# Borders between the sub-layers of a four-layer trunk on one core: order of conditioning and weight work, buffers of the last weights, engine of one split

## The chip, the cores and the metric

One core of a Trainium2 chip runs the whole program in one launch. The metric is the time of one execution on the device in microseconds (us). Engines are named as in the profile: PE (TensorE matmuls; PEld its weight loads), DVE (VectorE), ACT (ScalarE), POOL (GpSimd) and SP (the queue that issues the DMAs here).

## The reference

Four layers on x of 512 tokens by 1024 features. Each layer has two sub-layers f, a token mixer (convolution module, gated linear recurrence, matrix memory, stick-breaking attention, one kind per layer) and a gated ConvFFN with 2816 hidden features. Each is applied as

```
h = x * (1 + scale) + shift
x <- LayerNorm(alpha * x + (1 + gate) * f(h))
```

Shift, scale and gate are columns of `silu(c) @ ada_w[i] + ada_b[i]`, 6 x 1024 numbers for each layer, from one conditioning vector c. All is in fp32.

## The kernel before

The rows of x lie in four tiles X[0..3] of 128 tokens by 1024 (t is the row block). Precision comes from splitting each operand into a high part (`fp32r`, cast by ACT) and a low part (the difference, by DVE), and adding three products on PE: high*high, low*high, high*low.

**Weights.** `unit` (L223) loads one 512 KB piece of weights into one of three `raw` buffers by a DMA on SP, and `parts` (L239) splits it: ACT casts `whi` (L243), DVE subtracts `wlo` (L245). Both tags have WBUFS = 3 buffers for the whole program, so a fourth piece is cast only when PE is through with the first.

**The end of a sub-layer.** `down` (L317) is the last product. In its second half (h = 1) the last TAIL = 3 pieces are all loaded first (L362), and PE then goes row block by row block: 18 matmuls for t = 0, then for t = 1, 2 and 3, so that the norm of one row block runs while PE is at the next. For each row block `evict` (L556) does the norm: DVE adds the product to X (L567) and takes statistics (L568, L591, L592), POOL takes the power of -1/2 (L593), DVE finishes (L594), ACT normalises (L606, twice), and `make_h` (L484) makes the next sub-layer's h: PE transposes into PSUM (L492, tile `tr`, once for each half q of four 128-blocks), ACT (q = 0, L497) or DVE (q = 1, L500) applies scale and shift, ACT casts `hh` (L503), and the low part `hl` (L504) comes from POOL for q = 0 and from DVE for q = 1. The second norm of a layer and the first of the next are the same code, so there are seven such borders. The eighth end, the output, has no next sub-layer.

**The start of the next one.** The four FFNs and the matrix memory begin with `up_head` (L276): three pieces of weights, each multiplied first with the columns of t = 0 and 1 (24 matmuls of 256 columns), then, all three again, with those of t = 2 and 3. After them `up` (L286) takes one piece at a time. The recurrence and the attention begin with `down(..., head=HEAD)`, which takes t = 0, 1 of three pieces and then t = 2, 3. The recurrence ends in `down_late` (L368), a different form of the last product: one piece of each half is left for the end.

**Conditioning.** `ada_unit` (L204) loads one 512 KB piece of ada_w into a buffer of tag `araw` (four of them) and reduces it against silu(c) on DVE (L209); `fill` (L212) calls it, mostly once for each `up`. FFN 0 holds 56 such units, FFN 1 and 2 hold 48 each, for the layer after.

**Order.** A scheduler puts every engine's instructions into one fixed order before the run, by priorities (`unit` has a raised one), data dependences and a model of durations. An engine executes in that order, so an instruction whose operand is late holds up all that follows on its engine. `tc.issue_after(z)` adds an edge of order, without a semaphore, from z to each instruction traced in the block on z's engine; DMAs on SP are not bound by it.

Of the kernel before, what the change touches and what calls it, by code (L numbers as in the profile page):

```python
# [10 lines left out]
F32 = mybir.dt.float32  # L11
F32R = mybir.dt.float32r
AF = mybir.ActivationFunctionType
ALU = mybir.AluOpType
PSUM = bass.MemoryType.PSUM

P = 128
D = 1024
T = 512
KD = D // P  # L20
# [3 lines left out]
NF = D_FF // P  # L24
# [12 lines left out]
WPRIO = 150  # L37
# [11 lines left out]
FB = 4  # L49
WBUFS = 3  # L50
TAIL = 3
# [92 lines left out]
class Trunk:  # L144
    def __init__(self, ctx, tc, ins, out):
        self.ctx, self.tc, self.nc, self.ins, self.out = ctx, tc, tc.nc, ins, out
        nc = self.nc
        E = ctx.enter_context
        self.const = E(tc.tile_pool(name="const", bufs=1))
        self.wp = E(tc.tile_pool(name="wp", bufs=2))  # L150
        self.xp = E(tc.tile_pool(name="xp", bufs=1))
        self.sp = E(tc.tile_pool(name="sp", bufs=2))
        self.ps = E(tc.tile_pool(name="ps", bufs=1, space=PSUM))
        self.psum(mm="012345", tr="67")
        self.ident = self.const.tile([P, P], F32, name="ident")
        nc.sync.dma_start(out=self.ident, in_=ins["ident"])
        self.ones = self.const.tile([P, 1], F32, name="ones")
        nc.vector.memset(self.ones, 1.0)
        self.onesr = self.const.tile([P, P], F32R, name="onesr")
        nc.vector.tensor_copy(self.onesr, self.ones.broadcast_to([P, P]))  # L160
        self.mhalf = self.const.tile([P, 8], F32, name="mhalf")
        nc.vector.memset(self.mhalf, -0.5)
        self.sbc = self.const.tile([P, D], F32, name="sbc")
        cb = self.wp.tile([P, D], F32, tag="raw", bufs=3, name="cb")
        nc.sync.dma_start(out=cb, in_=ins["c"].broadcast_to([P, D]))
        nc.scalar.activation(out=self.sbc, in_=cb, func=AF.Silu)
        self.X = [self.xp.tile([P, D], F32, name=f"X{t}") for t in range(NT)]
        self.par = {}
        self.adac = {}
        self.ada_q = []  # L170
        self.pre = {}
        self.apool = None
        self.started = False
        self.due = None

    def load_x(self):
        for t in range(NT):
# [34 lines left out]
    def fill(self, n=1):  # L212
        for _ in range(n):
            if self.apool is not None and self.ada_q:
                self.ada_unit(self.apool, self.abufs)

    def flush(self, i, upto, pool=None, bufs=None):
        pool = pool or self.apool
# [1 line left out]
            self.ada_unit(pool, bufs or self.abufs)  # L220


    def unit(self, w, u, name, gate=None, rowc=None, pool=None, bufs=WBUFS, prio=WPRIO):  # L223

        nc = self.nc
        pool = pool or self.wp
        with self.tc.high_priority(offset=prio):
            raw = self.wp.tile([P, D], F32, tag="raw", bufs=3, name=f"r_{name}_{u}")
            nc.sync.dma_start(out=raw, in_=w[u])
            if gate is not None:  # L230
                r = raw.rearrange("p (a c) -> p a c", a=2)
                gr = gate.rearrange("p (a c) -> p a c", a=1).broadcast_to([P, 2, T])
                if rowc is None:
                    nc.vector.tensor_tensor(out=r, in0=r, in1=gr, op=ALU.mult)  # L234
                else:
                    nc.vector.scalar_tensor_tensor(out=r, in0=r, scalar=rowc, in1=gr, op0=ALU.mult, op1=ALU.mult)
            return self.parts(raw, f"{name}_{u}", pool, bufs)

    def parts(self, raw, name, pool=None, bufs=WBUFS):  # L239
        nc = self.nc  # L240
        pool = pool or self.wp
        hi = pool.tile([P, D], F32R, tag="whi", bufs=bufs, name=f"wh_{name}")
        nc.scalar.copy(hi, raw)  # L243
        lo = pool.tile([P, D], F32R, tag="wlo", bufs=bufs, name=f"wl_{name}")
        nc.vector.tensor_tensor(out=lo, in0=raw, in1=hi.bitcast(F32), op=ALU.subtract)  # L245
        return hi, lo

# [28 lines left out]
    def up_head(self, w, us, name):  # L276

        hl = {}
        for u in us:
            hl[u] = self.unit(w, u, name)  # L280
            self.pre[u] = self.bank(f"p_{name}_{u}")
            self.up_mm(self.pre[u], hl[u], 0, T // 2)
        for u in us:
            self.up_mm(self.pre[u], hl[u], T // 2, T)

    def up(self, w, u, name, fills=1):  # L286
        if u in self.pre:
            ps = self.pre.pop(u)
        else:
            hl = self.unit(w, u, name)  # L290
            ps = self.bank(f"p_{name}_{u}")
            self.up_mm(ps, hl, 0, T)
        self.fill(fills)
        return ps
# [19 lines left out]

        return act

    def down(self, w, nk, act, name, halves, evict, head=0, tail=0, gate=None, rowc=None, early=0, turn=None):  # L317

        npair = nk // 2

        def load(h, kp):
            return self.unit(w, h * npair + kp, name, None if gate is None else gate[:, h * T:(h + 1) * T], rowc)

        def mm(bank, h, t, kp, hl, first, last):
            for a in range(2):
                ah, al = act(2 * kp + a, h)  # L330
                ts_ = slice(t * P, (t + 1) * P)
                wh, wl = (z[:, a * T:(a + 1) * T] for z in hl)
                for n, (l, r) in enumerate(((ah, wh), (al, wh), (ah, wl))):
                    self.nc.tensor.matmul(bank, l[:, ts_], r, start=(kp == first and a == n == 0),  # L334
                                          stop=(kp == last and a == 1 and n == 2))

        if early:
            hls = [load(0, kp) for kp in range(early)]
            for t0 in (0, 2):
                banks = [self.bank(f"pe_{name}_{t0 + t}") for t in range(2)]  # L340
                for kp in range(early):
                    for t in range(2):
                        mm(banks[t], 0, t0 + t, kp, hls[kp], 0, early - 1)
                for t in range(2):
                    evict(0, t0 + t, banks[t], True)
            self.psum(**turn)
        for h in range(halves):
            banks = [self.bank(f"p_{name}_{h}_{t}") for t in range(NT)]
            k0 = early if h == 0 else 0
            nh = head if h == 0 else 0  # L350
            nt = tail if h == halves - 1 else 0
            end = npair - 1
            hls = [load(h, kp) for kp in range(k0, nh)]
            for t0 in (0, 2):
                for kp in range(k0, nh):
                    for t in (t0, t0 + 1):
                        mm(banks[t], h, t, kp, hls[kp], k0, end)
            for kp in range(max(nh, k0), npair - nt):
                hl = load(h, kp)
                for t in range(NT):  # L360
                    mm(banks[t], h, t, kp, hl, k0, end)
            hls = [load(h, kp) for kp in range(npair - nt, npair)]  # L362
            for t in range(NT):
                for q, kp in enumerate(range(npair - nt, npair)):
                    mm(banks[t], h, t, kp, hls[q], k0, end)
                evict(h, t, banks[t])
# [117 lines left out]
    def make_h(self, n, t, G, B, name):  # L484

        nc = self.nc
        ts_ = slice(t * P, (t + 1) * P)
        for q in range(2):
# [4 lines left out]
            hf = self.sp.tile([P, 4, P], F32, tag="u", bufs=4, name=f"hf_{name}_{t}_{q}")  # L493
            for j in range(4):
# [4 lines left out]
                else:  # L499
                    nc.vector.tensor_scalar(out=hf[:, j, :], in0=ps[:, j * P:(j + 1) * P], scalar1=G[:, k:k + 1],  # L500
                                            scalar2=B[:, k:k + 1], op0=ALU.mult, op1=ALU.add)
            hh = self.hh[:, 4 * q:4 * q + 4, ts_]
            nc.scalar.copy(hh, hf)  # L503
            (nc.gpsimd if q == 0 else nc.vector).tensor_tensor(out=self.hl[:, 4 * q:4 * q + 4, ts_], in0=hf,  # L504
                                                               in1=hh.bitcast(F32), op=ALU.subtract)

    def first_h(self, i, w=None, us=(), name=None):

# [100 lines left out]
    def conformer(self, nxt):  # L609
# [9 lines left out]
        with tc.tile_pool(name="cf", bufs=1, reuse_waits="tile") as op, ExitStack() as es, \  # L619
# [70 lines left out]
            nc.sync.dma_start(out=bias, in_=ins["bpw2"].broadcast_to([P, D]))  # L690
            gate, evict = self.sub_end(cf, i, 0, nxt, bias)
            act = self.ring(cf, us, "cu", keep=True)
            self.down(ins["pw2"], KD, act, "pw2", 2, evict, tail=TAIL, gate=gate)


    def hgrn(self, nxt):
# [215 lines left out]
    def mlstm(self, nxt):  # L912
# [7 lines left out]
        with tc.tile_pool(name="mx", bufs=1, reuse_waits="tile") as mp, \  # L920
# [200 lines left out]
            with tc.tile_pool(name="mb", bufs=1, reuse_waits="tile") as bp:  # L1121
                self.psum(mm="012345", tr="67")
                gate, evict = self.sub_end(bp, i, 0, nxt, gate=gate)
                self.down(ins["mdn"], NM, self.ring(bp, xc, "mu"), "mdn", 2, evict, tail=TAIL, gate=gate)


    def stick(self, nxt):
# [4 lines left out]
        with tc.tile_pool(name="so", bufs=1, reuse_waits="tile") as op, ExitStack() as es:  # L1132
# [152 lines left out]
            for _, n, p in sorted((p + o, n, p) for p in range(KD) for n, o in STEPS.items()):  # L1285
# [2 lines left out]
            op = es.enter_context(tc.tile_pool(name="sf", bufs=1, reuse_waits="tile"))  # L1288
            gate, evict = self.sub_end(op, i, 0, nxt, gate=gate)
            self.down(ins["swo"], KD, lambda k, h: so[k], "swo", 2, evict, tail=TAIL, gate=gate,  # L1290
                      early=3, turn=dict(mm="012345", tr="67"))


    def ffn(self, i, nxt):
# [3 lines left out]
        with tc.tile_pool(name=f"g{i}", bufs=1, reuse_waits="tile") as gp:  # L1298
# [25 lines left out]
            self.flush(99, 0)  # L1324
            self.apool = None
            gate, evict = self.sub_end(gp, i, 1, nxt, gate=gate)
            self.down(dn_w, NF, self.ring(gp, gs, f"gr{i}"), f"d{i}", 2, evict, tail=TAIL, gate=gate)


@with_exitstack  # L1330
# [45 lines left out]
```

## Time and profile before

| | |
|---|---|
| median of 3 runs | 2791.32 us (2790.43 to 2795.23) |
| the profiled execution's own time | 2790.0 us |
| its span, first to last instruction | 2788.2 us |
| granted TensorE clock, mean over the span | 0.985 |
| busy: PE, DVE, ACT, POOL | 96%, 73%, 46%, 3% of the span |

Matmuls overlap in the records: one of 128x512 is shown as 0.39 us long and the next starts 0.23 us after it. So idle time of PE in the rows is shorter than the time that a wait costs. In the rows below, the text in square brackets is the engine's idle time just before the instruction and what ended it.

### The profile page before, as it was taken

To read this page: it belongs to the slowest core of one execution; us is meant where nothing else is said; L and a number is where in the kernel's file an instruction comes from. 1 tells how busy PE (TensorE), PEld (TensorE's weight loads), DVE (VectorE), ACT (ScalarE), POOL (GpSimd) and SP (SyncE) were. 2 spreads that over 40 slices of the span, in tenths; PEclk is the share of its full clock that TensorE was granted. 3 is DMA by queue.
4 is the path that set the end of the run, shared out by engine and by line. 5 is a ranking of instruction groups with operands and counts; after the bars stand their busy time and mean duration, and the time that the engine had idled before them with its cause. 6 is when DMAs were issued, how large, how long until landed. Compare 5 with 4: busy or idle time off the path is not lost. (4 is left out here: it accounts for less than half of the span.)

```text
span 2788.2 us, 33764 instructions
## 1 busy us (share of the span) xinstructions
PE 2669.6 (96%) x12980; PEld 2135.8 (77%) x12980; DVE 2031.1 (73%) x3105; ACT 1270.1 (46%) x1773; POOL 90.2 (3%) x108
## 2 busy tenths in 40 slices
PE   7979999999998899999999999999999999999998
PEld 5537888877775688887887777888887777788886
DVE  7557997664777699576766776997666588666676
ACT  3133433335674443333555543543334798443332
POOL 0001000000000100000000000100001000100000
PEclk9989999999999899999999999999999999999999
DMA  9834874323221485322322222774333211233222
GB/s 323 228 107 151 288 239 140 99 83 101 86 72 46 145 289 189 99 94 82 104 86 68 91 84 83 264 257 136 98 99 96 66 48 37 98 99 113 95 95 76
DMA packets 109673, 352.33 MB, mean 126 GB/s; under 512 B 12104, under 2 KB 22600, under 8 KB 109512
## 3 DMA queue, kind: packets, MB, share of 16 engines
q1 hardware_dynamic: 109512, 350.17, 38.2%
q8 instruction: 102, 1.67, 0.3%
q14 instruction: 59, 0.48, 0.1%
HBM read 341.63 MB, written 8.50 MB: 126 GB/s over the span
## 5 line engine op out<-in xcount | busy, mean ns | idle before, releaser
L273 PE MATMUL p_f<-hl,wh_f 128*128 128x512 f32 (+1 forms) x1504 | 567.9, 378 | 8.8 <-POOL hl L504 8.8
L273 PE MATMUL p_f<-hh,wh_f 128*128 128x512 f32 (+1 forms) x1504 | 566.0, 378 | 5.5 <-ACT hh L503 5.5
L273 PE MATMUL p_f<-hh,wl_f 128*128 128x512 f32 (+1 forms) x1504 | 565.8, 377 | 0.0
L243 ACT CAST wh_f<-r_f 128x1024 fp32r<-128x1024 f32 x176 | 185.1, 1053 | 337.6 <-PE p_f L273 330.5
L273 PEld LDWEIGHTS p_f<-hl,wh_f 128*128 128x128 f32 x1504 | 285.1, 190 | 61.8 <-POOL hl L504 10.9
L273 PEld LDWEIGHTS p_f<-hh,wh_f 128*128 128x128 f32 x1504 | 284.4, 190 | 57.8 <-ACT hh L503 6.4
L273 PEld LDWEIGHTS p_f<-hh,wl_f 128*128 128x128 f32 x1504 | 284.9, 190 | 51.5 <-issue 0.2
L245 DVE TENSOR_TENSOR wl_f<-r_f,wh_f 128x1024 fp32r<-128x1024 f32 x176 | 217.3, 1236 | 144.1 <-ACT wh_f L243 143.2
L209 DVE CUSTOM_DVE_ANT_0 ada<-ada,sbc,adab 128x1024 f32<-128x1024 f32 x192 | 243.1, 1275 | 9.1 <-DMA ada<-in_ada_dram 9.0
L1308 DVE SCALAR_TENSOR_TENSOR cg<-p_f,par,cg 128x511 f32<-128x511 f32 (+1 forms) x176 | 130.9, 744 | 2.7 <-ACT cg L1306 1.4
L1308 DVE SCALAR_TENSOR_TENSOR cv<-p_f,par,cv 128x511 f32<-128x511 f32 (+1 forms) x176 | 130.9, 744 | 1.5
L234 DVE TENSOR_TENSOR r_d<-r_d,gate 128x1024 f32<-128x1024 f32 x88 | 107.5, 1222 | 28.2 <-DMA r_d<-in_fdn_dram 27.3
L245 DVE TENSOR_TENSOR wl_d<-r_d,wh_d 128x1024 fp32r<-128x1024 f32 x88 | 107.5, 1221 | 27.4 <-ACT wh_d L243 27.4
L1318 ACT ACTIVATE cg<-cg 128x512 f32<-128x512 f32 x88 | 55.4, 629 | 146.6 <-DVE cg L1308 144.5
L273 PE MATMUL p_mup<-hh,wh_mup 128*128 128x512 f32 (+1 forms) x280 | 109.4, 391 | 0.9 <-ACT hf L497 0.9
L273 PE MATMUL p_mup<-hl,wh_mup 128*128 128x512 f32 (+1 forms) x280 | 108.0, 386 | 0.6 <-POOL hl L504 0.6
L273 PE MATMUL p_mup<-hh,wl_mup 128*128 128x512 f32 (+1 forms) x280 | 108.4, 387 | 0.0
L243 ACT CAST wh_d<-r_d 128x1024 fp32r<-128x1024 f32 x88 | 92.2, 1048 | 32.7 <-PE p_f L273 16.7
L593 POOL TENSOR_TENSOR mv<-mv,mhalf 128x1 f32<-128x1 f32 x32 | 21.9, 683 | 1852.1 <-DVE mv L592 1851.3
L606 ACT ACTIVATE X<-X,mv 128x512 f32<-128x512 f32 x56 | 42.6, 810 | 84.2 <-DVE mv L594 84.2
L1306 ACT ACTIVATE cg<-p_f,par 128x512 f32<-128x512 f32 x88 | 68.1, 774 | 14.9 <-PE p_f L273 14.9
L334 PE MATMUL p_d<-wl_d,gr2h 128*128 128x512 f32 x176 | 69.6, 396 | 0.0
(511 smaller groups left out, 5966.0 us busy)
## 6 DMA issues: line engine op xcount, KB each, us to landing
ada<-in_ada_dram SPq DMA_DIRECT2D x192, 512.0 KB, 4.6
r_f<-in_fup_dram SPq DMA_DIRECT2D x176, 512.0 KB, 3.5
r_d<-in_fdn_dram SPq DMA_DIRECT2D x88, 512.0 KB, 3.3
r_mup<-in_mup_dram SPq DMA_DIRECT2D x32, 512.0 KB, 3.3
r_pw<-in_pw_dram SPq DMA_DIRECT2D x24, 512.0 KB, 7.7
r_hqf<-in_hqf_dram SPq DMA_DIRECT2D x16, 512.0 KB, 3.3
r_mdn<-in_mdn_dram SPq DMA_DIRECT2D x16, 512.0 KB, 3.3
r_sqk<-in_sqk_dram SPq DMA_DIRECT2D x16, 512.0 KB, 3.7
```

Of the source, the lines that this page charges most:

```text
L209: nc.vector.tensor_tensor_reduce(out=raw, in0=raw, in1=self.sbc, scale=1.0, scalar=ab[:, j:j + 1], op0=ALU.mult, op1=ALU.add, accum_out=ac ...
L234: nc.vector.tensor_tensor(out=r, in0=r, in1=gr, op=ALU.mult)
L243: nc.scalar.copy(hi, raw)
L245: nc.vector.tensor_tensor(out=lo, in0=raw, in1=hi.bitcast(F32), op=ALU.subtract)
L273: self.nc.tensor.matmul(ps[:, c0:c1], a, b[:, k, c0:c1], start=(n == 0), stop=(n == 3 * KD - 1))
L334: self.nc.tensor.matmul(bank, l[:, ts_], r, start=(kp == first and a == n == 0), stop=(kp == last and a == 1 and n == 2))
L593: nc.gpsimd.tensor_tensor(out=mv[:, 2:3], in0=mv[:, 1:2], in1=self.mhalf[:, 0:1], op=ALU.pow)
L606: nc.scalar.activation(out=o[:, hs], in_=x[:, hs], func=AF.Identity, scale=mv[:, 2:3], bias=mv[:, 3:4])
L1306: nc.scalar.activation(out=o, in_=ps, func=AF.Identity, scale=w[2], bias=par[:, C_CONVB + m:C_CONVB + m + 1])
L1308: nc.vector.scalar_tensor_tensor(out=o[:, s:], in0=ps[:, :T - s], scalar=w[2 - s], in1=o[:, s:], op0=ALU.mult, op1=ALU.add)
L1318: nc.scalar.activation(out=cg, in_=cg, func=AF.Silu)
```

## The change

Four edits. (1) `make_h` does both low halves `hl` on DVE, and keeps the last cast and the last subtraction as `self.chain`. (2) `behind` opens `issue_after` for both; `fill` traces its ada units in it, and `up` the first three weight pieces that it splits itself after `up_head` (`late = 3`). So these are ordered on ACT and DVE after the last `make_h` step of the sub-layer before. (3) `down` takes `spare`: of the three tail pieces the second and third put their high and low parts into buffers of their own, in the FFNs the four `araw` buffers of 4 KB for each partition, in the convolution module, the matrix memory and the attention four new ones of tag `tw`. `down_late` has none. (4) `parts` takes the allocator `into` for that.

```diff
     def fill(self, n=1):
         for _ in range(n):
             if self.apool is not None and self.ada_q:
-                self.ada_unit(self.apool, self.abufs)
+                with self.behind():
+                    self.ada_unit(self.apool, self.abufs)
+    @contextmanager
+    def behind(self):
+        with ExitStack() as es:
+            for z in self.chain or ():
+                es.enter_context(self.tc.issue_after(z.ins))
+            yield
...
-        hi = pool.tile([P, D], F32R, tag="whi", bufs=bufs, name=f"wh_{name}")
+        tile_ = into or (lambda tag, nm: pool.tile([P, D], F32R, tag=tag, bufs=bufs, name=nm))
+        hi = tile_("whi", f"wh_{name}")
         nc.scalar.copy(hi, raw)
-        lo = pool.tile([P, D], F32R, tag="wlo", bufs=bufs, name=f"wl_{name}")
+        lo = tile_("wlo", f"wl_{name}")
...
         for u in us:
             self.up_mm(self.pre[u], hl[u], T // 2, T)
+        self.late = 3
     def up(self, w, u, name, fills=1):
...
-            hl = self.unit(w, u, name)
+            if self.late:
+                self.late -= 1
+                with self.behind():
+                    hl = self.unit(w, u, name)
+            else:
+                hl = self.unit(w, u, name)
...
-            hls = [load(h, kp) for kp in range(npair - nt, npair)]
+            hls = [load(h, kp, spare if kp > npair - nt else None) for kp in range(npair - nt, npair)]
...
-            nc.scalar.copy(hh, hf)
-            (nc.gpsimd if q == 0 else nc.vector).tensor_tensor(out=self.hl[:, 4 * q:4 * q + 4, ts_], in0=hf,
-                                                               in1=hh.bitcast(F32), op=ALU.subtract)
+            a = nc.scalar.copy(hh, hf)
+            b = nc.vector.tensor_tensor(out=self.hl[:, 4 * q:4 * q + 4, ts_], in0=hf, in1=hh.bitcast(F32), op=ALU.subtract)
+            self.chain = a, b
...
-            self.down(dn_w, NF, self.ring(gp, gs, f"gr{i}"), f"d{i}", 2, evict, tail=TAIL, gate=gate)
+            self.down(dn_w, NF, self.ring(gp, gs, f"gr{i}"), f"d{i}", 2, evict, tail=TAIL, gate=gate,
+                      spare=lambda tag, nm: gp.tile([P, D], F32R, tag="araw", bufs=FB, name=nm))
```

## Rows read from the trace of the kernel before

**Rows 1.** The page's first part: busy time and share of the span.
```profile
PE 2669.6 (96%) x12980; PEld 2135.8 (77%) x12980; DVE 2031.1 (73%) x3105; ACT 1270.1 (46%) x1773; POOL 90.2 (3%) x108
```
**Rows 2.** 40 us around each border: busy PE, PEld, DVE, ACT, POOL; PEclk; DMA.
```profile
238.00:278.00 40.00, 34.43 (x216) 30.32 (x215) 30.09 (x56) 21.41 (x38) 9.65 (x8) 0.96 0.49 171
614.00:654.00 40.00, 37.48 (x176) 29.50 (x175) 27.36 (x72) 24.60 (x41) 7.90 (x8) 1.00 0.26 82
931.00:971.00 40.00, 30.79 (x174) 26.73 (x174) 36.07 (x69) 18.45 (x34) 11.45 (x8) 0.83 0.54 183
1310.00:1350.00 40.00, 34.69 (x204) 30.14 (x203) 24.96 (x54) 21.44 (x38) 8.11 (x9) 0.91 0.20 65
1731.00:1771.00 40.00, 34.70 (x229) 30.45 (x229) 31.19 (x58) 22.86 (x39) 9.64 (x8) 1.00 0.50 174
2105.00:2145.00 40.00, 37.48 (x177) 29.80 (x176) 26.39 (x56) 23.68 (x40) 7.97 (x8) 1.00 0.28 84
2392.00:2432.00 40.00, 36.44 (x239) 32.08 (x238) 26.66 (x50) 25.11 (x42) 7.87 (x8) 1.00 0.27 94
```
**Rows 3.** Waits of PE, whole span: us in total, times, longest us.
```profile
PE tr L492 <- ACT X L606: 17.4, 20, 2.5
PE p_f L273 <- POOL hl L504: 8.8, 8, 1.6
PE p_f L273 <- ACT hh L503: 5.5, 4, 2.3
...
PE p_mup L273 <- ACT hf L497: 0.9, 1, 0.9
...
PE p_mup L273 <- POOL hl L504: 0.6, 1, 0.6
```
**Rows 4.** Timeline of PE at the fifth border: start us, length us.
```profile
1735.14 0.66 PE L492 MATMUL tr<-ident,X 128*128 128x128 f32 x4 [0.44 <-ACT X L606]
...
1741.22 0.39 PE L334 MATMUL p_mdn<-wh_mdn,muh 128*128 128x512 f32 x1
1741.45 0.40 PE L334 MATMUL p_mdn<-wh_mdn,mul 128*128 128x512 f32 x1
1742.73 0.66 PE L492 MATMUL tr<-ident,X 128*128 128x128 f32 x4 [0.89 <-ACT X L606]
...
1747.42 0.28 PE L273 MATMUL p_f<-hh,wh_f 128*128 128x256 f32 x1
1748.32 0.39 PE L273 MATMUL p_f<-hl,wh_f 128*128 128x256 f32 x1 [0.62 <-POOL hl L504]
...
1757.95 0.66 PE L492 MATMUL tr<-ident,X 128*128 128x128 f32 x4 [0.93 <-ACT X L606]
...
1760.85 0.62 PE L273 MATMUL p_f<-hh,wh_f 128*128 128x256 f32 x3 [0.83 <-ACT hh L503]
1763.08 0.38 PE L273 MATMUL p_f<-hl,wh_f 128*128 128x256 f32 x1 [1.60 <-POOL hl L504]
```
**Rows 5.** Timeline of DVE in the same stretch.
```profile
1747.37 1.98 DVE L245 TENSOR_TENSOR wl_f<-r_f,wh_f 128x1024 fp32r<-128x1024 f32 x1 [0.24 <-PE p_mdn L334]
...
1749.88 1.21 DVE L245 TENSOR_TENSOR wl_f<-r_f,wh_f 128x1024 fp32r<-128x1024 f32 x1
1751.01 0.68 DVE L567 SCALAR_TENSOR_TENSOR X<-X,p_mdn 128x512 f32<-128x512 f32 x1
...
1755.17 1.27 DVE L209 CUSTOM_DVE_ANT_0 ada<-ada,sbc,adab 128x1024 f32<-128x1024 f32 x1
```
**Rows 6.** The low halves, all borders: duration ns min/median/max.
```profile
L504 POOL TENSOR_TENSOR hl<-hf,hh x28: 1275/1298/2559, 245.8 to 2421.0; 128x512 fp32r<-128x512 f32 x28
L504 DVE TENSOR_TENSOR hl<-hf,hh x28: 632/1273/1779, 246.3 to 2421.5; 128x512 fp32r<-128x512 f32 x28
```
**Rows 7.** Busy time in two stretches of FFN 0, as in rows 2.
```profile
300.00:400.00 100.00, 100.00 (x443) 82.81 (x442) 98.10 (x137) 39.53 (x51) 0.00 (x0) 1.00 0.81 273
...
450.00:500.00 50.00, 50.00 (x218) 40.69 (x217) 31.96 (x43) 18.45 (x25) 0.00 (x0) 1.00 0.28 93
```

More of the change, by code (lines that the diff above doesn't have):

```diff
@@ L174, in __init__ @@
         self.due = None
+        self.chain = None
+        self.late = 0
     def load_x(self):
@@ L220, in flush, with unit @@
             self.ada_unit(pool, bufs or self.abufs)
-    def unit(self, w, u, name, gate=None, rowc=None, pool=None, bufs=WBUFS, prio=WPRIO):
+    def unit(self, w, u, name, gate=None, rowc=None, pool=None, bufs=WBUFS, prio=WPRIO, into=None):
         nc = self.nc
@@ L236, in unit, with parts @@
                     nc.vector.scalar_tensor_tensor(out=r, in0=r, scalar=rowc, in1=gr, op0=ALU.mult, op1=ALU.mult)
-            return self.parts(raw, f"{name}_{u}", pool, bufs)
-    def parts(self, raw, name, pool=None, bufs=WBUFS):
+            return self.parts(raw, f"{name}_{u}", pool, bufs, into)
+    def parts(self, raw, name, pool=None, bufs=WBUFS, into=None):
         nc = self.nc
         pool = pool or self.wp
-        hi = pool.tile([P, D], F32R, tag="whi", bufs=bufs, name=f"wh_{name}")
+        tile_ = into or (lambda tag, nm: pool.tile([P, D], F32R, tag=tag, bufs=bufs, name=nm))
+        hi = tile_("whi", f"wh_{name}")
         nc.scalar.copy(hi, raw)
-        lo = pool.tile([P, D], F32R, tag="wlo", bufs=bufs, name=f"wl_{name}")
+        lo = tile_("wlo", f"wl_{name}")
         nc.vector.tensor_tensor(out=lo, in0=raw, in1=hi.bitcast(F32), op=ALU.subtract)
@@ L315, in ring, with down, load @@
         return act
-    def down(self, w, nk, act, name, halves, evict, head=0, tail=0, gate=None, rowc=None, early=0, turn=None):
+    def down(self, w, nk, act, name, halves, evict, head=0, tail=0, gate=None, rowc=None, early=0, turn=None, spare=None):
         npair = nk // 2
-        def load(h, kp):
-            return self.unit(w, h * npair + kp, name, None if gate is None else gate[:, h * T:(h + 1) * T], rowc)
+        def load(h, kp, into=None):
+            return self.unit(w, h * npair + kp, name, None if gate is None else gate[:, h * T:(h + 1) * T], rowc, into=into)
         def mm(bank, h, t, kp, hl, first, last):
@@ L692, in conformer @@
             act = self.ring(cf, us, "cu", keep=True)
-            self.down(ins["pw2"], KD, act, "pw2", 2, evict, tail=TAIL, gate=gate)
+            self.down(ins["pw2"], KD, act, "pw2", 2, evict, tail=TAIL, gate=gate,
+                      spare=lambda tag, nm: cf.tile([P, D], F32R, tag="tw", bufs=4, name=nm))
     def hgrn(self, nxt):
@@ L1123, in mlstm @@
                 gate, evict = self.sub_end(bp, i, 0, nxt, gate=gate)
-                self.down(ins["mdn"], NM, self.ring(bp, xc, "mu"), "mdn", 2, evict, tail=TAIL, gate=gate)
+                self.down(ins["mdn"], NM, self.ring(bp, xc, "mu"), "mdn", 2, evict, tail=TAIL, gate=gate,
+                          spare=lambda tag, nm: bp.tile([P, D], F32R, tag="tw", bufs=4, name=nm))
     def stick(self, nxt):
@@ L1290, in stick @@
             self.down(ins["swo"], KD, lambda k, h: so[k], "swo", 2, evict, tail=TAIL, gate=gate,
-                      early=3, turn=dict(mm="012345", tr="67"))
+                      early=3, turn=dict(mm="012345", tr="67"),
+                      spare=lambda tag, nm: op.tile([P, D], F32R, tag="tw", bufs=4, name=nm))
     def ffn(self, i, nxt):
```

## The prediction, made before the changed kernel was run

> **What bounds the kernel now.** I read the page's first part, then busy time by stretch, then what PE waits for, then the timelines of PE and DVE at one border. PE is busy for 96% of the span [rows 1], so a change that leaves its matmuls alone can only pay where PE stands idle. Each of the seven 40 us stretches around a border holds such time: 40 less PE's busy time is 5.57, 2.52, 9.21, 5.31, 5.30, 2.52 and 3.56 us, together 34.0 us [rows 2]. The page's busy time leaves much more idle over the span, but that lies in the convolution module, the recurrence and the last norm, which this change hardly touches.
>
> The waits name the releasers [rows 3]: transposes wait 17.4 us for the normalised X, the first products of the next sub-layer 9.4 us for POOL's `hl` (8.8 + 0.6) and 6.4 us for ACT's `hh` and `hf` (5.5 + 0.9). Twenty transposes waited. Six of them belong to t = 0, of about 0.44 us as at 1735.14, and seven to t = 1, of about 0.89 us as at 1742.73 [rows 4]; that is 2.6 + 6.2 = 8.8 us. The other seven are of t = 3, as at 1757.95, and have 17.4 - 8.8 = 8.6 us.
>
> An idle time of 0.89 us costs more than that: from 1741.45 to 1742.73 there are 1.28 us where the step before is 0.23 us, so 1.05 us are lost [rows 4], 0.16 us more than the record shows. And three borders run partly at half clock: PEclk 0.96, 0.83 and 0.91 of 40 us are 1.6 + 6.8 + 3.6 = 12.0 us [rows 2]. Two borders with waits like these kept 1.00, so the clock is a consequence that does not follow each time.
>
> **Why t = 3 is late: the fifth border.** PE is through with the tail at 1747.42, where its first `p_f` matmul stands [rows 4]; but DVE takes the product of t = 3 into X only at 1751.01, because two splits of the next sub-layer's weights (1747.37, slowed to 1.98 us, and 1749.88, 1.21 us) are ahead of it [rows 5]. These splits stand there because the three tail pieces hold all three buffers until the last row block. Then a conditioning unit of 1.27 us (1755.17) runs between the steps of t = 3's norm [rows 5]. PE gets the first `hl` at 1763.08 [rows 4].
>
> **The change, part by part.**
>
> *Own buffers for two tail pieces.* They release two weight buffers when the last piece ahead of the tail is done, 18 x 4 matmuls of 0.23 us = 16.6 us before the tail ends. So two of the three splits go ahead of the norms of t = 1 to 3; DVE's free 27% of the span [rows 1] hides them there, and without that cover they would cost up to 2 x 1.21 us each border. The third stays: its buffer comes free only in t = 3's own matmuls. DVE takes t = 3's product 1751.01 - 1747.42 = 3.6 us earlier if none is in the way and 2.4 us if the third split (1.21 us) still is. I take 3.
>
> *Conditioning behind the last step.* It removes 1.27 us from t = 3's chain [rows 5]. The units run after it; what hides them is DVE's idle time until the fourth weight piece is split, and later slack: DVE is 98% busy from 300 to 400 us but has 18.0 of 50 us free from 450 to 500 us, ahead of the end of FFN 0's up product [rows 7]. Five or six units of 1.27 us are 6.4 to 7.6 us: covered. Were the cover gone, that is the price at each of the three borders with conditioning, 23 us at most. On SP, an ada DMA waits for its buffer and the weight DMAs issued behind it wait too; three raw buffers are filled ahead of that, so I take 0, and one unit's 1.27 us at three borders as the bound. Ordering the next weights by `late` I put at 0 as well: the fourth piece needs a buffer that PE frees only with its second half of `up_head`, later than the chain's end. A gain or loss of up to one split, 1.2 us, at five borders is its bound.
>
> *Low halves on DVE.* The 28 subtractions of POOL took 1.298 us at the median and 2.559 at most, those of DVE 0.632 at best and 1.273 at the median [rows 6]. Without POOL beside it I take 0.64 for each of the two: both are done 1.28 us after they can start, and the first, which PE needs first, after 0.64 instead of 1.3 to 2.15. Gain on the chain: 0.7 to 1.5 us, I take 1.0. DVE's own total stays: 28 x 1.27 = 36 us before, 56 x 0.64 = 36 after. The Trainium skill ("SBUF — State Buffer", Who interferes with whom) says that a DVE instruction with two SBUF operands and a GpSimd instruction that reads SBUF exclude each other for a whole instruction. By that rule the addition to DVE's load is nothing, as here; without it, it would be 28 x 0.64 = 18 us.
>
> *What is late next.* At the fifth border t = 3's `hl` comes 3 + 1.27 + 1.0 = 5.3 us earlier, at about 1757.8. PE's own work ahead of that product runs from 1747.42 to 1760.85 with 0.62 + 0.93 + 0.83 us idle [rows 4]; without these it ends at 1758.5. So PE becomes the later of the two, by 0.7 us: the waits go, with little to spare. I leave 0.5 us at each of the five `up_head` borders.
>
> **The sum.** Removable: 8.6 (t = 3) + 9.4 (`hl`) + 6.4 (`hh`, `hf`) = 24.4 us. Staying: 5 x 0.5 = 2.5 us, and at the third border, which ends in the form without own buffers, the longest `hh` wait of 2.3 us and some 0.5 of `hl`, as ACT and DVE still split weights there. That makes 19.1 us. Some 19 waits fewer, 0.16 us each, are 3.0 us. Of the 12.0 us of half clock about 3.4 hang on the wait that stays, and half-clock time partly coincides with waiting; between 0 and 8.6 us I take 4. Together 26 us: 2790.0 - 26 = 2764 us for an execution like the profiled one. The median of the runs is 1.3 us above that one: **2765 us**.
>
> Its own range: all waits removable, 24.4 + 3.5 + 8.6 = 36.5 us, gives 2755; half of the t = 3 and `hh` waits left and no clock regained gives 9.4 + 7.5 + 2 = 19 us, 2772.
>
> **Rivals.**
> 1. *The norm of t = 3 stays the last to arrive* (chance 0.18). The third split and the order that the scheduler fixes still hold up t = 2 and t = 3, since DVE now has both low halves. Then only the `hl` waits go and a quarter of the t = 3 waits: 9.4 + 2.2 + some hidden 1 = 12.6 us, 2779. For it: DVE is busy for 36.07 of 40 us at the third border [rows 2]. Against it: 24.96 to 31.19 of 40 at the other `up_head` borders.
> 2. *It does not do what it says* (0.07). The splits of the next weights stay where they are, since priorities and the model of durations decide, or the raw buffers hold them up; less than 5.6 us is gained: about 2789. Against it: the free `whi` buffer, not the raw one, is what these splits wait for, and three raw buffers suffice for the three pieces.
> 3. *DVE becomes the bound at the border* (0.06), the slower side. If the subtraction moved from POOL is ordered ahead of the statistics of the next row block, each of t = 1, 2 and 3 comes 0.64 us later: 3 x 7 x 0.64 = 13.4 us, 2804 us if nothing is gained elsewhere. It decides where DVE has no idle time between two row blocks and its old `hl` was not slowed by POOL. Against it: 0.632 against 1.273 us [rows 6]; the single subtraction already takes the time of two. The Trainium skill ("Perfetto Trace Analysis", Optimizing Scalar/DVE Operations) advises handing work to ScalarE or GpSimd where DVE is saturated, the opposite of this edit; it adds that the port shared by GpSimd and DVE may undo that, and the rows are on this side.
>
> **How the numbers follow.** Forecast 0.69, rivals 0.18, 0.07, 0.06. The range reaches from a little under all removable waits, 2754, past the first rival, to 2784; the other two and the ends left out make up about 0.2. A measurement here tells 0.2%, 5.6 us, from no change: faster 0.87 (the forecast and the first rival), within 0.2% 0.07, slower 0.06.
>
> **What would show it.** In the profile after: no `hl` on POOL and all 56 on DVE near 0.64 us; two of the next sub-layer's splits ahead of the first norm step; no conditioning on DVE before the last `hl`; PE's wait for `hl` near 0 and for `tr` down to about 9 to 11 us; PE busy for 38 of 40 us around the borders with `up_head` but the third, where 34 to 36 stay; PEclk 1.00 at the first and fourth. It would be wrong if the waits of t = 0 and 1 grow by what those of t = 3 lose, if weight splits still stand between t = 2 and t = 3 on DVE, or if PE gets new waits inside the FFNs' up products.

## The result and the profile after

The changed kernel takes 2759.98 us (median of 4 runs, 2756.47 to 2761.82), the one before 2792.06 us on the same chip; the ratio is 0.9882, 95% interval 0.9867 to 0.9896. That is 32 us gained where 26 were forecast (2765 us, range 2754 to 2784). Run again with the last experiment it took 2760.08 us, ratio 0.9894 (0.9878 to 0.9911), 29 us less than the kernel before on that chip. One execution of a later run, `s_pool`, was slow at 9297.12 us; it counts in that run's median and not in its ratio.

The profiled execution took 2756.47 us, the fastest of the four; its span is 2754.6 us. The page's first part answers to [rows 1]: POOL's busy time is halved and its 28 subtractions are gone, and PE's matmuls are the same in number.

```profile
PE 2655.6 (96%) x12980; PEld 2128.7 (77%) x12980; DVE 2027.7 (74%) x3133; ACT 1270.9 (46%) x1773; POOL 43.7 (2%) x80
```

The same 40 us around each border, columns as in [rows 2] (busy PE, PEld, DVE, ACT, POOL; PEclk; DMA):

```profile
236.00:276.00 40.00, 38.08 (x249) 33.90 (x248) 30.64 (x62) 23.27 (x40) 2.20 (x4) 1.00 0.44 151
608.00:648.00 40.00, 38.90 (x183) 30.68 (x182) 25.17 (x74) 24.20 (x42) 2.20 (x4) 1.00 0.20 65
923.00:963.00 40.00, 36.27 (x229) 32.92 (x228) 35.32 (x71) 25.16 (x42) 2.65 (x4) 0.91 0.48 168
1292.00:1332.00 40.00, 37.03 (x241) 32.37 (x240) 26.26 (x62) 23.26 (x42) 2.75 (x5) 1.00 0.17 52
1706.00:1746.00 40.00, 38.17 (x249) 33.87 (x248) 31.22 (x63) 23.27 (x40) 2.21 (x4) 1.00 0.45 158
2076.00:2116.00 40.00, 38.65 (x184) 30.84 (x183) 24.14 (x58) 22.45 (x39) 2.20 (x4) 1.00 0.21 67
2361.00:2401.00 40.00, 38.14 (x249) 33.83 (x248) 26.76 (x55) 25.07 (x42) 2.20 (x4) 1.00 0.21 78
```

PE's idle time is 1.92, 1.10, 3.73, 2.97, 1.83, 1.35 and 1.86 us, together 14.8 us where 34.0 stood. The half clock is gone at the first and fourth border and halved at the third: (1 - PEclk) x 40 us, the time lost to it, sums to 3.6 us instead of 12.0. What PE waits for at the borders (total us, times, longest), where [rows 3] stood:

```profile
PE tr L512 <- ACT X L626: 12.2, 22, 2.1
...
PE p_f L285 <- ACT hh L523: 1.5, 1, 1.5
...
PE p_mup L285 <- ACT hf L517: 0.9, 1, 0.9
```

No wait for `hl` is left. DVE at the fifth border, in the order of time, answers to [rows 5]:

```profile
1697.32 1.23 DVE L257 TENSOR_TENSOR wl_f<-r_f,wh_f 128x1024 fp32r<-128x1024 f32 x1 [0.26 <-ACT wh_f L255]
...
1702.88 1.23 DVE L257 TENSOR_TENSOR wl_f<-r_f,wh_f 128x1024 fp32r<-128x1024 f32 x1 [3.73 <-ACT wh_f L255]
1706.15 0.69 DVE L587 SCALAR_TENSOR_TENSOR X<-X,p_mdn 128x512 f32<-128x512 f32 x1 [2.05 <-PE p_mdn L354]
...
1720.62 1.23 DVE L257 TENSOR_TENSOR wl_f<-r_f,wh_f 128x1024 fp32r<-128x1024 f32 x1
1721.76 1.29 DVE L524 TENSOR_TENSOR hl<-hf,hh 128x512 fp32r<-128x512 f32 x2
1722.97 0.68 DVE L587 SCALAR_TENSOR_TENSOR X<-X,p_mdn 128x512 f32<-128x512 f32 x1
...
1732.18 1.30 DVE L524 TENSOR_TENSOR hl<-hf,hh 128x512 fp32r<-128x512 f32 x2
1733.39 1.28 DVE L211 CUSTOM_DVE_ANT_0 ada<-ada,sbc,adab 128x1024 f32<-128x1024 f32 x1
```

Two splits of the next weights run before the first norm step (1706.15), the third split is still in the middle (1720.62), and conditioning begins after the last `hl`. PE in the same stretch:

```profile
1709.81 0.66 PE L512 MATMUL tr<-ident,X 128*128 128x128 f32 x4 [0.48 <-ACT X L626]
...
1717.45 0.66 PE L512 MATMUL tr<-ident,X 128*128 128x128 f32 x4 [0.51 <-ACT X L626]
...
1721.66 0.52 PE L285 MATMUL p_f<-hh,wh_f 128*128 128x256 f32 x3
1722.39 0.66 PE L512 MATMUL tr<-ident,X 128*128 128x128 f32 x4 [0.21 <-ACT X L626]
...
1729.29 0.66 PE L512 MATMUL tr<-ident,X 128*128 128x128 f32 x4 [0.63 <-ACT X L626]
```

From the end of the tail to t = 3's first finished `hl` there were 1763.08 - 1747.42 = 15.7 us [rows 4]; now 1732.18 + 0.65 - 1721.66 = 11.2 us. The waits that are left are those of the transposes and, at the third and fourth border, one each for `hh` and `hf`. Counted over the same 320 PE instructions around each border, from the 60th before its first transpose on, the seven borders took 458.1 us before and 430.1 us now (430.0 in the profile of the second run), 28 us less.

### The profile page after: what moved, and what is told of

It is laid out like the page before. It is cut to its first block, busy times and chain, and to the rows that moved or that the text cites. A ratio compares the mean times of both kernels' runs of the same rounds, so it can differ in the third digit from the quotient of the medians.

```text
span 2754.6 us, 33739 instructions
## 1 busy us (share of the span) xinstructions
PE 2655.6 (96%) x12980; PEld 2128.7 (77%) x12980; DVE 2027.7 (74%) x3133; ACT 1270.9 (46%) x1773; POOL 43.7 (2%) x80
## 4 chain that ended last, share of the span: by engine, by line
PE 79%; DVE 9%; ACT 8%; DMA 2%; issue 2%; POOL 1%; SPq 0%; POOLq 0%; DVEq 0%; ACTq 0%
PE p_f L285 34%; PE p_d L354 16%; PE p_mup L285 5%; PE p_pw L285 3%; PE p_mdn L354 3%; PE p_hqf L285 2%; PE p_hv L354 1%; PE p_sv L354 1%; PE pc L683 1%; PE p_pw L354 1%; PE p_hg L285 1%; PE p_hwo L406 1%; PE ms L977 1%; PE tr L512 1%; ACT hf L517 1%
## 5 line engine op out<-in xcount | busy, mean ns | idle before, releaser
L1329 ACT ACTIVATE cv<-p_f,par 128x512 f32<-128x512 f32 x88 | 68.1, 774 | 3.9 <-PE p_f L285 3.9
```

What stands on the lines that cost most here:

```text
L1329: nc.scalar.activation(out=o, in_=ps, func=AF.Identity, scale=w[2], bias=par[:, C_CONVB + m:C_CONVB + m + 1])
```

## The experiments

Three edits, each alone and in pairs, give all eight combinations (the pairs keep `late`, the single edits do not; `u_late` below shows it to be worth nothing). After each median stands the ratio to the kernel before on the same chip, with its 95% interval. First the whole change with one edit taken out.

**Without own buffers** (`u_spare`)
```diff
-            hls = [load(h, kp, spare if kp > npair - nt else None) for kp in range(npair - nt, npair)]
+            hls = [load(h, kp) for kp in range(npair - nt, npair)]
```


> The change without the tail's own buffers; its other parts stay. If the buffers are what lets t = 3's norm start on time, two splits of 1.05 us (ACT) and 1.23 us (DVE) come back between the norms of t = 2 and t = 3 at six borders: about 2.4 us later each, so some 14 us slower than the whole change, near 2774 us. Rival: DVE was held up by conditioning and by the low halves and the buffers count for little; then within 4 us of 2760.

2764.85 us, 0.9911 (0.9898 to 0.9925): about 5 us lost, not 14. All three splits are back among the norms at the fifth border, and t = 3's product reaches X after them at 1730.30:

```profile
1725.04 1.22 DVE L257 TENSOR_TENSOR wl_f<-r_f,wh_f 128x1024 fp32r<-128x1024 f32 x1
1726.82 1.23 DVE L257 TENSOR_TENSOR wl_f<-r_f,wh_f 128x1024 fp32r<-128x1024 f32 x1
1727.96 1.29 DVE L524 TENSOR_TENSOR hl<-hf,hh 128x512 fp32r<-128x512 f32 x2
1729.17 1.22 DVE L257 TENSOR_TENSOR wl_f<-r_f,wh_f 128x1024 fp32r<-128x1024 f32 x1
1730.30 0.68 DVE L587 SCALAR_TENSOR_TENSOR X<-X,p_mdn 128x512 f32<-128x512 f32 x1
```

So the mechanism is there, and most of its price is not: t = 3's transposes wait 0.65 us, as in the whole change (0.63). What PE loses at this border it loses earlier, at the start of `up_head`, where t = 1's `hh` and `hl` stand behind the first two splits:

```profile
1727.36 0.51 PE L285 MATMUL p_f<-hh,wh_f 128*128 128x256 f32 x2 [0.27 <-ACT hh L523]
1728.70 0.39 PE L285 MATMUL p_f<-hl,wh_f 128*128 128x256 f32 x1 [0.84 <-DVE hl L524]
...
1736.61 0.66 PE L512 MATMUL tr<-ident,X 128*128 128x128 f32 x4 [0.65 <-ACT X L626]
```

**Without conditioning behind** (`u_ada`)
```diff
-                with self.behind():
-                    self.ada_unit(self.apool, self.abufs)
+                self.ada_unit(self.apool, self.abufs)
```


> The change with conditioning no longer queued behind the last step. Only the borders into FFN 0, 1 and 2 have such units. Expected: 1.3 to 2.5 us at each of the three and some half clock at the third, 4 to 8 us slower than the whole change, near 2766. Rival: with DVE freed by the buffers the units fit into its idle time; no difference, 2760.

2767.14 us, 0.9916 (0.9902 to 0.9929): about 7 us lost, as expected.

**Low half of q = 0 on POOL again** (`u_pool`)
```diff
-            b = nc.vector.tensor_tensor(out=self.hl[:, 4 * q:4 * q + 4, ts_], in0=hf, ...)
+            b = (nc.gpsimd if q == 0 else nc.vector).tensor_tensor(out=self.hl[:, 4 * q:4 * q + 4, ts_], in0=hf, ...)
```


> The change with the low half of q = 0 back on POOL. Expected: the first product of the next sub-layer waits again for POOL (0.64 against 1.3 to 2.1 us), 0.7 to 1.5 us at seven borders: 5 to 10 us slower than the whole change, near 2767. Rival (DVE is the bound at the border): 0.64 us faster at each of three row blocks, down to 2747.

2767.22 us, 0.9913 (0.9899 to 0.9926): about 7 us lost; the wait for POOL is back, and DVE is not the bound:

```profile
PE p_f L285 <- POOL hl L524: 3.7, 4, 1.6
```

**Without `late`** (`u_late`)
```diff
-        self.late = 3
```


> The change with the next three weight pieces not queued behind the last step. Expected: no difference, 2760 within 2 us, as the fourth piece needs a buffer that PE frees only in the second half. Rival: with two buffers free early the scheduler had put one of these pieces into the norms; then 3 to 6 us slower.

2759.2 us, 0.9887 (0.9873 to 0.99): no difference from the whole change. Its row in the code does nothing for the time.

The three losses add up to 19 of some 30 us, so each edit was then put alone into the kernel before.

**Own buffers alone** (`s_spare`: the edits of `u_pool`, `u_ada` and `u_late` together)

> The kernel before with the tail's own buffers alone. Taking the buffers out of the whole change cost only about 5 us. If the three parts shorten one chain against a fixed amount of PE work, each alone does more than its removal showed: about 10 us gained, near 2781 us (t = 3's product reaches X some 2.4 us earlier at six borders). Rival, parts that add up: 5 us gained, near 2786. Second rival, parts that need each other: under 3 us.

2774.13 us, 0.9944 (0.9932 to 0.9955): 15 us gained, more than any of the expectations. The first, third, fourth and fifth border (columns as above):

```profile
235.00:275.00 40.00, 36.41 (x242) 32.53 (x241) 30.92 (x61) 21.30 (x38) 8.74 (x8) 1.00 0.46 162
...
926.00:966.00 40.00, 30.78 (x176) 26.91 (x175) 35.30 (x69) 18.79 (x35) 11.44 (x8) 0.83 0.55 185
1303.00:1343.00 40.00, 36.68 (x242) 32.47 (x241) 27.45 (x58) 23.15 (x42) 8.70 (x9) 1.00 0.16 52
1716.00:1756.00 40.00, 36.52 (x241) 32.46 (x240) 31.48 (x61) 22.13 (x39) 8.74 (x8) 1.00 0.48 167
```

The third, which has no own buffers, is as before (9.2 us idle, 0.83). The first and fourth lose 2.0 of their idle time each and all of their half clock, 5.2 us by [rows 2]; the fifth loses 1.8 us of idle time. The second, sixth and seventh, which have own buffers too, keep theirs within 0.2 us: three borders gain, not six.

**Conditioning behind, alone** (`s_ada`: the edits of `u_pool`, `u_spare` and `u_late` together)

> The kernel before with conditioning queued behind the last step alone (its removal cost about 7 us). One chain: 7 to 10 us gained at the borders into FFN 0, 1 and 2, near 2782, with the half clock of the first and third border shorter. Parts that add up: 7 us, 2784. Parts that need each other: under 4 us.

2778.25 us, 0.9957 (0.9945 to 0.9969): 11 us gained. Only the borders that have conditioning change, the third most:

```profile
236.00:276.00 40.00, 36.10 (x238) 32.02 (x238) 29.49 (x55) 23.23 (x40) 7.87 (x8) 1.00 0.43 150
...
926.00:966.00 40.00, 35.01 (x226) 31.50 (x224) 34.11 (x65) 24.22 (x41) 8.65 (x8) 0.91 0.46 157
1296.00:1336.00 40.00, 34.70 (x202) 30.00 (x201) 24.29 (x54) 20.77 (x37) 8.13 (x9) 0.91 0.19 65
1717.00:1757.00 40.00, 36.33 (x239) 31.96 (x238) 29.40 (x55) 23.14 (x40) 7.88 (x8) 1.00 0.43 147
```

Idle falls by 1.7, 4.2 and 1.6 us at the first, third and fifth; the fourth is as before.

**Both low halves on DVE, alone** (`s_pool`: the edits of `u_spare`, `u_ada` and `u_late` together)

> The kernel before with both low halves on DVE alone (its removal cost about 7 us). One chain: 7 to 10 us gained, near 2782. Parts that add up: 7 us. DVE as the bound while weight splits and conditioning are still there: no gain or slower, 2790 to 2796.

2781.8 us, 0.9970 (0.9958 to 0.9982): 8 us gained. DVE's subtractions, with the splits and the conditioning still among them, take half of what they took beside POOL [rows 6]:

```profile
L522 DVE TENSOR_TENSOR hl<-hf,hh x56: 671/685/694, 243.7 to 2408.6; 128x512 fp32r<-128x512 f32 x56
```

Alone the edits gain 15 + 11 + 8 = 34 us, together about 30, and their removals cost 5 + 7 + 7 = 19: in time they overlap, the buffers most. The profiles show where. Sums over the seven stretches of 40 us, as after the result:

| kernel | PE idle, us | lost to half clock, us |
|---|---|---|
| before | 34.0 | 12.0 |
| own buffers alone | 28.3 | 6.8 |
| conditioning alone | 26.4 | 7.2 |
| low halves alone | 25.8 | 6.8 |
| whole change without own buffers | 18.6 | 3.6 |
| whole change without conditioning | 19.2 | 5.2 |
| whole change without low halves | 24.0 | 3.6 |
| whole change | 14.8 | 3.6 |

In PE's idle time the parts nearly add up: 5.7 + 7.6 + 8.2 = 21.5 us alone, 19.2 together, 3.8 + 4.4 + 9.2 = 17.4 by removal. In the half clock they do not: 5.2 + 4.8 + 5.2 = 15.2 us alone, 8.4 together, 0 + 1.6 + 0 by removal. So most of the overlap is half clock: each edit alone brings back about five of the 8.4 us. One chain shortened against a fixed amount of PE work, which the expectations had, explains at most the small rest.

**Own buffers for the recurrence's last two pieces** (`i_rec`)
```diff
-        hls = [[load(h, kp) for kp in left[h]] for h in range(2)]
+        hls = [[load_halves(h, kp, ...) for kp in left[h]] for h in range(2)]
```
(`load_halves` does what `unit` does, in two halves of 512 columns into tiles of the tags KD, E, B and QD, sT.)

> The whole change, and the recurrence's last two pieces of weights in buffers of their own too (split in halves of 512 columns, in eight tiles that the recurrence is through with). If the third border keeps its 3.7 us idle and 6.8 us of half clock because weight splits stand among its norms, these go down by 2 to 3 us each: 3 to 5 us faster than the whole change, near 2756. Rival: the border is short of PE work for t = 0 to 2, as its tail is only 12 matmuls per row block; no difference.

2759.95 us, 0.9891 (0.9878 to 0.9903): no difference. The splits are gone from the norms (the last is at 926.95, the first norm step at 928.09), but PE waits as long as in the whole change, 1.88 + 1.54 us against 2.14 + 1.54:

```profile
938.93 1.36 PE L529 MATMUL tr<-ident,X 128*128 128x128 f32 x8 [1.88 <-ACT X L643]
941.83 1.01 PE L285 MATMUL p_f<-hh,wh_f 128*128 128x256 f32 x3 [1.54 <-ACT hh L540]
```

The weight splits are not what holds this border up. That PE has too little work beside the norms there, 12 matmuls for each row block instead of 18, fits but was not tested by itself.

**Transposes of t = 0 later** (`i_tr`, and again as `i_tr2` next to the whole change, `after2`)
```diff
+TRAT = {0: 34}
...
+                        if done[0] in pend:
+                            with self.tc.issue_after(z.ins):
+                                pend.pop(done[0])()
...
-                evict(h, t, banks[t])
+                fin = evict(h, t, banks[t])
+                if fin is not None:
+                    if t in TRAT:
+                        pend[TRAT[t]] = fin
+                    else:
+                        fin()
```
(`done` counts the tail's 72 matmuls; `fin` is `make_h`.)

> The whole change, and the transposes of t = 0 ordered behind the 16th of the 18 matmuls of t = 1 instead of the 13th or 14th, where PE waits 0.48 us for them at six borders. If the waits that are left come from the place that the scheduler gave the transposes in PE's order, two matmuls of 0.23 us move in front: 0.46 us each, some 2.8 us in all, near 2757 us, and the wait of t = 0 down to about 0.05 us. Rival: the norm of t = 1 hangs on the same steps and PE waits there instead; no difference, 2760.

2753.1 us, 0.9879 (0.9862 to 0.9897). PE's wait for the transposes falls from 12.2 us in 22 waits to 6.0 in 13, more than was expected, as those of t = 1 and 3 get shorter too:

```profile
PE tr L527 <- ACT X L645: 6.0, 13, 2.1
```

> The whole change again, next to the version with the later transposes: 2760 us within 2 us.

> The later transposes of t = 0 again, on the same chip as the whole change. The borders lost 5.5 us less in the first profile of it: 4 to 7 us faster than the whole change, 2753 to 2756. Rival: the first run fell on favourable clocks outside the borders; then within 3 us of the whole change.

2760.08 us for the whole change, 2757.0 (0.9883, 0.9868 to 0.9897) for this version beside it: 3 to 7 us faster by the two medians, but the intervals overlap, so the medians do not settle the gain. The profiles do, for the borders: PE's idle time in the seven stretches is 9.5 and 9.8 us in the two runs where the whole change has 14.8, with the same 3.6 us lost to half clock; over the same 320 PE instructions each, the seven borders took 425.4 and 425.5 us instead of 430.1. The two spans still differ by 7.3 us (2748.6 and 2755.9): their mean granted clocks, 0.990 and 0.987, make about 8 us of difference, all of it outside the borders. So the rival of favourable clocks is right about what the first run gained beyond some 5 us. At the fifth border the transposes of t = 0 wait for nothing and those of t = 1 for 0.32 us.

```profile
1713.19 1.36 PE L527 MATMUL tr<-ident,X 128*128 128x128 f32 x8
1720.61 0.66 PE L527 MATMUL tr<-ident,X 128*128 128x128 f32 x4 [0.32 <-ACT X L645]
```

## Why the prediction was right, and where its sizes were off

- *PE's idle time at the borders is what can be gained.* Right: 19.1 us were to go, 34.0 - 14.8 = 19.2 went, and no new wait of PE stands in the FFNs' up products. By [rows 3] 5.2 us of the transposes' waits, all 9.4 us for `hl` and 4.0 us for `hh` and `hf` went.
- *Some 19 waits fewer, 3.0 us.* Too large: the 34 waits of [rows 3] became 24, ten fewer, 1.6 us at 0.16 us each.
- *Half clock: 4 us, between 0 and 8.6.* Too small: 12.0 - 3.6 = 8.4 us came back. This is the largest part of the 6 us between forecast and result. Most of the rest is luck of the clock outside the borders. By mean granted clock and span the half clock there cost about 30 us before, 27 in the profile shown of the changed kernel and 32 in its other one (mean 0.985, 0.989 and 0.987, spans 2788.2, 2754.6 and 2758.7 us). The borders themselves gained 28 us in both.
- *Own buffers: t = 3 some 3 us earlier.* By the rows, DVE took t = 3's product 3.6 us after the tail's end and now 1722.97 - 1721.66 = 1.3 us: 2.3 us, just under the lower end given, since the third split stays. Of the 15 us that the buffers give alone, 5.2 are half clock that the other edits bring back as well, so leaving them out of the whole change costs only 5 us.
- *Conditioning: 1.27 us at three borders.* Too small, and not the way it was said. Alone it took 1.7, 4.2 and 1.6 us of idle time and part of the half clock. At the fifth border the unit at 1755.17 did not cost t = 3's norm its own length: DVE was idle again after it, waiting for POOL's power of -1/2, which took 1.46 us beside the unit and 0.55 us for t = 2. Another unit, at 1760.63, ran beside POOL's `hl`, which took 2.15 us where the median is 1.298 [rows 6]. At the third border six units stood among the steps of t = 2 and 3. DVE and POOL in the kernel before, at the fifth:

```profile
1756.89 0.16 DVE L594 SCALAR_TENSOR_TENSOR mv<-mv 128x1 f32<-128x1 f32 x1 [0.43 <-POOL mv L593]
...
1760.63 1.27 DVE L209 CUSTOM_DVE_ANT_0 ada<-ada,sbc,adab 128x1024 f32<-128x1024 f32 x1
```
```profile
1743.74 0.55 POOL L593 TENSOR_TENSOR mv<-mv,mhalf 128x1 f32<-128x1 f32 x1 [2.10 <-DVE mv L592]
...
1755.40 1.46 POOL L593 TENSOR_TENSOR mv<-mv,mhalf 128x1 f32<-128x1 f32 x1 [0.76 <-DVE mv L592]
1760.88 2.15 POOL L504 TENSOR_TENSOR hl<-hf,hh 128x512 fp32r<-128x512 f32 x1 [4.02 <-ACT hh L503]
```

- *Low halves: 1.0 us a border, DVE's total unchanged.* Right: 0.689 us each after, 56 x 0.689 = 39 us where 36 stood, and about 8 us alone or 7 us last for seven borders.
- *`late` at nothing*: right, within the intervals.
- *The third border keeps 2.3 + 0.5 us because weights are still split among its norms.* It kept 3.7 us, but not for that reason: `i_rec` took the splits out and the waits stayed.
- *t = 1's transposes keep their 0.89 us.* They fell to about 0.51 us, but at the third border they rose from 0.98 to 2.14 us. Transposes wait 12.2 us where 9 to 11 were said, since t = 3's keep 2.8 us and t = 2's have new waits of 1.2 us together.
- *A sign of being wrong.* One came out by its letter: a weight split still stands between t = 2 and t = 3 on DVE (1720.62). It is the third, which the working itself has staying; the two that were to go ahead went (1697.32, 1702.88).

Rival 1 (the norm of t = 3 stays the last to arrive) is half true: its transposes still wait 0.63 us at the fifth border, but the `hh` and `hl` waits behind them are gone. Rivals 2 and 3 fell: the first norm has two splits ahead of it, and DVE with both low halves is faster in every combination.

## What to carry to other kernels

At a border between stages, list what stands in the queues of the engines that run the border's chain: work that is needed only later (conditioning, weight splits) can cost there even when the engine has idle time over the stage; at the third border moving the splits gained nothing. Edits can overlap, here mostly in half clock that each alone brings back, so measure them alone and last, and split the gain into waits and clock, before saying what one is worth. Where a fixed order makes the bound engine wait at a known place, moving the waiting instruction back by the length of the wait fills it with work that is there anyway.

## What the runs showed of the hardware

A subtraction of 128x512 on POOL and one on DVE at the same time took about as long as both on DVE in a row: 1.298 and 1.273 us at the median side by side [rows 6], 2 x 0.689 us after. In the kernel before, POOL's power of 128x1 took 1.46 to 1.52 us at t = 3 of the three borders with conditioning, beside a DVE unit of some 1.27 us, and 0.55 to 0.56 us at its 25 other places in the borders. And short waits cost twice at some borders. At the fourth border before, PE waited twice:

```profile
1337.15 1.36 PE L492 MATMUL tr<-ident,X 128*128 128x128 f32 x8 [2.47 <-ACT X L606]
1339.41 0.58 PE L273 MATMUL p_mup<-hh,wh_mup 128*128 128x256 f32 x1 [0.89 <-ACT hf L497]
```

The clock fell to 1.2 GHz at 1338.6 us, at the start of the second wait, and stayed there for 6.8 us (PEclk 0.50 from 1338.60 to 1345.40). After 0.93 + 0.83 + 1.60 us of waits at the fifth [rows 4] it did not fall, and in the changed kernel it fell only at the third of the seven borders. With the low halves alone (`s_pool`) the fifth border was idle for less than before, 4.77 us instead of 5.30, and yet its PEclk was 0.96 instead of 1.00. What decides it between such waits is not shown.
